# A two-layer SSD / HGRN2 trunk: TensorE's order in the SSD stage written out by hand, diagonal products of two tiles in one run, output projections in halves

## The chip, the cores and the metric

The kernel runs on one core of a Trainium2 chip. The metric is the device time of one execution in microseconds (us), as the median of several runs. Four engines matter here: TensorE (PE in the profile; its weight loads are a row of their own, PEld), VectorE (DVE), ScalarE (ACT) and SyncE (SP), which issues the transfers. Each engine has its own queue of instructions; they wait for each other through semaphores.

## What is computed

The reference is a trunk of two layers over 512 tokens with 1024 features. Layer 0 mixes the tokens with a Mamba-2 SSD mixer, layer 1 with an HGRN2 mixer; each mixer is followed by a layer norm, a squared-ReLU MLP, another layer norm and a gated embedding. The change touches the SSD mixer alone, which is, cut to what matters:

```python
zxbcdt = u @ w_in                                  # z 2048, x 2048, B 512, C 512, dt 32
xbc = silu(causal_depthwise_conv(xbc, conv_w, conv_b))     # x, B and C
dt = softplus(dt + dt_bias); da = dt * -exp(a_log); a_cs = cumsum(da, within a chunk of 128)
decay = segsum_exp(da); xdt = xs * dt
y_diag = einsum(C B^T, decay, xdt)                 # inside a chunk
states = einsum(B, exp(a_cs[last] - a_cs), xdt)    # what a chunk hands on
prev = scan(h * chunk_decay + states)              # over the 4 chunks
y_off = einsum(C, prev, exp(a_cs))                 # what comes from earlier chunks
y = (y_diag + y_off + d_skip * xs) * silu(z)
y = rms_norm(y, over each of 4 groups of 512 features)
return y @ w_out
```

There are 4 groups of 8 heads with 64 features each. B and C belong to a group, everything else to a head.

## The kernel before

**Numbers.** A large product is taken three times (`mm3`, L119 to L121: high by high, high by low, low by high part), each a matmul with 512 columns. Every weight block of 128 x 1024 (a unit) is loaded by SP into `raw`, rounded to its high part by ACT (L113, `whi`) and subtracted to its low part by DVE (L115, `wlo`). Small products (transposes, states, diagonal and carried parts) are single float32 products; each of them is two rows in the profile, except that a transpose is one.

**Tiles of the SSD stage.** The 2048 features are 16 tiles of 128, that is two heads each, and four tiles make a group. For each group there are two projections for B and C (`bc_group`), whose outputs go through the convolution (`conv_silu`, ACT L631, three DVE steps on L634, ACT L635), and `bc_prep`, which transposes B (L660) and forms C B^T masked (TensorE L666, DVE L668, in bank py0). For each tile `xz` makes two projections, x (convolved) and z (Silu, L683). A projection is 8 steps of `mm3`, 24 matmuls. Then `core` does, for one tile:

- the load of its cumulative sums, `csb` (L689), and four transposes of x (L693), which DVE scales to `xw` (L700) and `xdt` (L701);
- the states, three products (L705) into bank pm, and from them the carried states `pv`, a chain of five DVE operations (L712, then L714 and L715 twice), with a chunk decay from ACT (L709);
- the decay matrix `m`: eight DVE steps (L721), an exponential on ACT (L724), a product with C B^T on DVE (L725);
- the diagonal part, eight products (L735) that are 64 output rows wide, into bank py0;
- the carried part, three products (L741) into bank py1;
- y: DVE L748 to L751, then its high part on ACT (L800), its low part on DVE (L801), and the sum of squares (L756, L759).

`rms_group` (L762 to L772) turns a group's sum of squares into the factor `ri`; its products (L767) are 64 x 64. `out_project` multiplies a finished group by its part of the output weights: two halves of 512 output features, four token chunks each, 12 matmuls for each of these eight parts, and DVE adds each part to `acc` (L253).

**What sets the order.** The loop at L783 is written tile by tile: projections of tile j, then `core` of tile j-1, and for some tiles the whole output projection of the group before. That is only the order of priority: on all engines in the SSD stage, TensorE too, a scheduler at compile time decides what goes next, by its own reckoning of when operands are there, and it may put a small product between any two `mm3` matmuls. Two later stages already have TensorE's order written by hand (`manual_schedule`): the value projections and the HGRN2 core.

**Banks and buffers.** PSUM has eight banks here: four take turns for large products (pj), one is for transposes and the group sums (pt), and py0, py1 and pm are single. In the SSD stage x and z tiles have two buffers each, `xdt`, `ecs` and `y` one.

The start (a load of x and of the first four weight blocks, and dt) and everything after the SSD stage is the same in both kernels.

Of the kernel before, what the change touches and what calls it, by code (L numbers as in the profile page):

```python
# [15 lines left out]
P = 128  # L16
# [28 lines left out]
def trunk(ctx: ExitStack, tc, a):  # L45
# [25 lines left out]
    def f32(t):  # L71
        return t.bitcast(F32)

    two = dict(xs=2, sz=2, cv=2, cm=2, cbm=2)
    mlp = dict(r=8, blk=2, sg=2)
    bufs = dict(ssd=dict(two, ss=2), mlp0=mlp, hgrn=dict(two, xs=4, sz=4, cv=4, y=2, pv=2, btok=2, sc=2, scb=2, qd=2), mlp1=mlp)
    phase = []

    def begin(name):
# [539 lines left out]
    def dt_tail():  # L619
# [5 lines left out]
        nc.vector.tensor_copy(t, pt[:, : 3 * P].rearrange("p (i c h) -> p i c h", i=3, c=NCH))  # L625
        return t[:, 0], t[:, 2], t[:, 1]

    def conv_silu(ps, i, out):
# [10 lines left out]
    def projected(i):  # L639

        if i < 4:
            return first[i]
        ps = bank(psj, "pj")
        project(unit(wssd[i - 4]), x_s, ps)
        return ps

    def bc_group(g):
        bcm = []
        for which in range(2):
            ps = projected(10 * g + which)  # L650
            t = tmp(("bm", "cm")[which], [P, T])
            conv_silu(ps, 16 + 4 * which + g, t)
            bcm.append(t)
        return bcm

    def bc_prep(bcm):
# [5 lines left out]
        nc.scalar.copy(btok, pt[:, : 3 * P].rearrange("p (c n) -> p c n", c=3))  # L662
        pc = bank(psy, "py0")
        for c in range(NCH):
            sl = slice(c * P, (c + 1) * P)
            nc.tensor.matmul(pc[:, sl], bm[:, sl], cm[:, sl], start=True, stop=True)  # L666
        cbm = tmp("cbm", [P, T])
        nc.vector.tensor_mul(  # L668
            cbm.rearrange("p (c l) -> p c l", c=NCH), pc.rearrange("p (c l) -> p c l", c=NCH), bc(triu, 1, NCH)
        )  # L670
        return btok, cbm, cm

    toks = []

    def xz(j):
        ps = projected(10 * (j // 4) + 2 + 2 * (j % 4))
        xs = tmp("xs", [P, T])
        conv_silu(ps, j, xs)
        if j == 1:
            toks.extend(dt_tail())  # L680
        ps = projected(10 * (j // 4) + 3 + 2 * (j % 4))
        sz = tmp("sz", [P, T])
        nc.scalar.activation(sz, ps, AF.Silu)  # L683
        return xs, sz

    def core(j, xs, sz, y, toks, btok, cbm, cm, ss=None):
        dt_tok, w_tok, cs_tok = toks
        csb = mk(w4, [P, 2, T], "a")
        nc.sync.dma_start(csb, bass.AP(tensor=csd.tensor, offset=csd.offset + 2 * j * T, ap=[[0, P], [T, 2], [1, T]]))  # L689

        pt = bank(pst, "pt")
        for c in range(NCH):
            nc.tensor.transpose(pt[:, c * P : (c + 1) * P], xs[:, c * P : (c + 1) * P], ident)  # L693
        xdt = tmp("xdt", [P, 8, 64])
        v = pt.rearrange("p (c h q) -> p (c h) q", c=NCH, h=2)
        xdt4 = xdt.rearrange("p (c h) q -> p c h q", c=NCH)
        hs = slice(2 * j, 2 * j + 2)
        ptv = pt.rearrange("p (c h q) -> p c h q", c=NCH, h=2)
        xw = tmp("xw", [P, 3, 2, 64])
        nc.vector.tensor_mul(xw, ptv[:, 0:3], bc(w_tok[:, 0:3, hs], 3, 64))  # L700
        nc.vector.tensor_mul(xdt4, ptv, bc(dt_tok[:, :, hs], 3, 64))  # L701

        pst_ = bank(psm, "pm")
        for c in range(3):
            nc.tensor.matmul(  # L705
                pst_[:, c * P : (c + 1) * P], btok[:, c, :], xw[:, c].rearrange("p h q -> p (h q)"), start=True, stop=True
            )
        cd = mk(sm, [P, 2, NCH], "cd")
        nc.scalar.activation(cd, csb.rearrange("p h (c l) -> p h c l", c=NCH)[:, :, :, P - 1], AF.Exp)  # L709
        pv = tmp("pv", [P, 3, 2, 64])  # L710
        stv = pst_[:, : 3 * P].rearrange("p (c h q) -> p c h q", c=3, h=2)
        nc.vector.tensor_copy(pv[:, 0], stv[:, 0])  # L712
        for c in range(1, 3):
            nc.vector.tensor_mul(pv[:, c], pv[:, c - 1], bc(cd[:, :, c], 2, 64))  # L714
            nc.vector.tensor_add(pv[:, c], stv[:, c], pv[:, c])  # L715

        m = mk(w4, [P, 2, T], "b")
# [9 lines left out]
        ecs = tmp("ecs", [P, 3 * P])  # L727
        for r in range(2):
            rs = slice(64 * r, 64 * r + 64)
            nc.scalar.activation(ecs[rs], csb[rs, r, P:], AF.Exp)  # L730
        yd = bank(psy, "py0")
        for c in range(NCH):
            sl = slice(c * P, (c + 1) * P)
            for r in range(2):
                nc.tensor.matmul(  # L735
                    yd[64 * r : 64 * r + 64, sl], xdt[:, 2 * c + r, :], m[:, r, sl], start=True, stop=True
                )
        ri = None if ss is None else rms_group(ss)
        yo = bank(psy, "py1")
        for c in range(1, NCH):  # L740
            nc.tensor.matmul(  # L741
                yo[:, c * P : (c + 1) * P],
                pv[:, c - 1].rearrange("p h q -> p (h q)"),
                cm[:, c * P : (c + 1) * P],
                start=True,
                stop=True,
            )
        nc.vector.scalar_tensor_tensor(y, xs, dskip[:, j : j + 1], yd, ALU.mult, ALU.add)  # L748
        nc.vector.tensor_mul(ecs, yo[:, P:], ecs)
        nc.vector.tensor_add(y[:, P:], y[:, P:], ecs)  # L750
        nc.vector.tensor_mul(y, y, sz)  # L751
        return ri

    def sq_sum(y, ss):
        sq = tmp("ss" if ss is None else "sq", [P, T])
# [16 lines left out]
        nc.vector.reciprocal(ri, ri)  # L772
        return ri

    def ssd_out(g, s, ri, *after):
        out_project(a["wso"][4 * g : 4 * g + 4], s, False, *after, scale=ri)

    pend = None
    ys = None
    bcm = None  # L780
    prep = None
    outs = []
    for j in range(17):  # L783
        nbcm = bc_group(j // 4) if j % 4 == 0 and j < 16 else None
        cur = xz(j) if j < 16 else None
        if j == 4:
            nc.sync.dma_start(acc, a["x"])
            for c in range(NCH):
                nc.vector.tensor_scalar(acc[:, c, :], acc[:, c, :], ALPHA, None, ALU.mult)
        if pend is not None:  # L790
            i = j - 1
            if i % 4 == 0:
                ys = Split(4)
                ss = None
                prep = bc_prep(bcm)
            y = tmp("y", [P, T])
            due = bool(outs) and (i % 4 == 1 or i == 15) and i != 13
            ri = core(i, *pend, y, toks, *prep, outs[0][2] if due else None)
            w = snw[:, i : i + 1]
            nc.scalar.activation(ys.h(i % 4), y, AF.Copy, scale=w)  # L800
            nc.vector.scalar_tensor_tensor(ys.l(i % 4), y, w, f32(ys.h(i % 4)), ALU.mult, ALU.subtract)  # L801
            ss = sq_sum(y, ss)
            if i % 4 == 3:
                outs.append((i // 4, ys, ss))
            if due:
                ssd_out(*outs.pop(0)[:2], ri)
        if nbcm is not None:
            bcm = nbcm
        pend = cur
# [431 lines left out]
```

## Time and profile before

| | |
|---|---|
| median of 3 runs (lowest, highest) | 1425.94 us (1425.18, 1426.01) |
| the profiled execution's own time | 1424.0 us |
| span in it, from first to last instruction | 1422.2 us |
| granted TensorE clock | 1.000 |
| DVE, ACT busy, share of the span | 74%, 53% |
| DMA read | 174.54 MB, 124 GB/s over the span |

How to read the profile. A row of the timeline has the start, the length, the engine, the line, the operation, the tile written and the tiles read, the sizes, and a count where neighbouring rows of one kind are merged. An idle time before the row stands in brackets with what ended it. Lengths of neighbouring rows overlap, since an engine takes the next instruction while the last is still on its way; what an instruction costs is therefore read from the distance of two starts, not from its length. A busy TensorE is not a TensorE at its peak.

### The profile page before, as it was taken

Reading aid. Unit: us, or ns where it says so; the run is one execution under the profiler, and the core shown is the slowest. Engines: PE = TensorE matmul, PEld = TensorE weight load, DVE = VectorE, ACT = ScalarE, POOL = GpSimd, SP = SyncE. Lnnn points to the kernel's source line nnn. Section 1 sums busy time; section 2 is a strip of 40 time slices with the busy share of each in tenths; the row PEclk is TensorE's granted clock in tenths of the full one; section 3 lists DMA queues with packets and bytes.
Section 4 is the critical chain, followed back from the end, with each engine's and each line's share of the span. In section 5 each row is a group of like instructions: output and inputs, shape, how many; then the busy total and the mean of one; then the engine's idle time right before and its main releaser. Section 6 shows DMA issues by size and latency. Waiting matters only on the chain.

```text
span 1422.2 us, 20042 instructions
## 1 busy us (share of the span) xinstructions
PE 1412.7 (99%) x7869; PEld 1172.5 (82%) x7869; DVE 1055.1 (74%) x1736; ACT 754.2 (53%) x1134; POOL 1.9 (0%) x12
## 2 busy tenths in 40 slices
PE   9999999999999999999999999999999999999998
PEld 7888888888888888888888888877898888888887
DVE  8998687797966767677986576678695867667873
ACT  7776454563265454545545556655555444544641
POOL 0000000000000000000000000000000000000000
PEclk9999999999999999999999999999999999999999
DMA  8432323233333434344621421222163444434231
GB/s 313 138 124 90 120 87 121 102 115 127 145 119 120 161 133 149 133 146 166 214 83 49 133 90 60 75 90 90 46 236 104 148 140 142 149 133 163 89 119 45
DMA packets 49390, 178.00 MB, mean 125 GB/s; under 512 B 5520, under 2 KB 6288, under 8 KB 49168
## 3 DMA queue, kind: packets, MB, share of 16 engines
q1 hardware_dynamic: 49296, 176.73, 36.3%
q8 instruction: 62, 1.02, 0.3%
q14 instruction: 32, 0.26, 0.1%
HBM read 174.54 MB, written 2.16 MB: 124 GB/s over the span
## 4 chain that ended last, share of the span: by engine, by line
PE 94%; DVE 2%; ACT 2%; DMA 1%; issue 0%; ACTq 0%; DVEq 0%
PE pj L119 24%; PE pj L120 24%; PE pj L121 24%; PE py L119 5%; PE py L121 5%; PE py L120 5%; PE py L735 1%; PE pt L233 1%; PE py L741 1%; PE pm L705 1%; DMA raw<-in_wssd 1%; PE py L972 1%; PE pt L693 1%; PE py L1078 1%; DVE wlo L115 0%
## 5 line engine op out<-in xcount | busy, mean ns | idle before, releaser
L113 ACT CAST whi<-raw 128x1024 fp32r<-128x1024 f32 x222 | 232.9, 1051 | 323.5 <-PE pj L120 225.1
L119 PE MATMUL pj<-b,whi 128*128 128x512 f32 (+1 forms) x1006 | 382.3, 381 | 0.7 <-ACT b L237 0.7
L120 PE MATMUL pj<-b,whi 128*128 128x512 f32 (+1 forms) x1006 | 380.3, 378 | 0.0
L121 PE MATMUL pj<-b,wlo 128*128 128x512 f32 (+1 forms) x1006 | 379.3, 377 | 0.0
L115 DVE TENSOR_TENSOR wlo<-raw,whi 128x1024 fp32r<-128x1024 f32 x222 | 270.0, 1221 | 126.4 <-ACT whi L113 124.6
L119 PEld LDWEIGHTS pj<-b,whi 128*128 128x128 f32 x1006 | 188.8, 188 | 34.2 <-ACT b L237 0.9
L121 PEld LDWEIGHTS pj<-b,wlo 128*128 128x128 f32 x1006 | 189.1, 188 | 33.7
L120 PEld LDWEIGHTS pj<-b,whi 128*128 128x128 f32 x1006 | 189.2, 188 | 32.8 <-issue 0.9
L119 PE MATMUL pj<-whi,b 128*128 128x512 f32 x536 | 213.0, 398 | 0.0
L121 PE MATMUL pj<-whi,b 128*128 128x512 f32 x544 | 212.9, 392 | 0.0
L120 PE MATMUL pj<-wlo,b 128*128 128x512 f32 x536 | 210.2, 392 | 0.0
L121 PEld LDWEIGHTS pj<-whi,b 128*128 128x128 f32 x544 | 102.1, 188 | 21.0
L119 PEld LDWEIGHTS pj<-whi,b 128*128 128x128 f32 x536 | 100.7, 188 | 20.7 <-ACT b L1099 0.6
L120 PEld LDWEIGHTS pj<-wlo,b 128*128 128x128 f32 x536 | 100.8, 188 | 19.3
L113 ACT CAST whi<-r 128x1024 fp32r<-128x1024 f32 x72 | 75.8, 1053 | 67.7 <-PE pj L121 38.6
L115 DVE TENSOR_TENSOR wlo<-r,whi 128x1024 fp32r<-128x1024 f32 x72 | 87.7, 1220 | 20.6 <-ACT whi L113 19.9
L121 PE MATMUL py<-whi,b 128*128 128x512 f32 (+1 forms) x250 | 97.0, 388 | 0.0
L120 PE MATMUL py<-wlo,b 128*128 128x512 f32 x224 | 87.1, 389 | 0.0
L119 PE MATMUL py<-whi,b 128*128 128x512 f32 x224 | 87.1, 390 | 0.0
L121 PEld LDWEIGHTS py<-whi,b 128*128 128x128 f32 x250 | 46.9, 188 | 9.7
L634 DVE SCALAR_TENSOR_TENSOR cv<-pj,cst,cv 128x509 f32<-128x509 f32 (+2 forms) x66 | 48.7, 745 | 3.5 <-ACT cv L631 2.8
L119 PEld LDWEIGHTS py<-whi,b 128*128 128x128 f32 x224 | 42.0, 188 | 9.1 <-DVE sg L494 0.3
(292 smaller groups left out, 1850.8 us busy)
## 6 DMA issues: line engine op xcount, KB each, us to landing
raw<-in_w SPq DMA_DIRECT2D x112, 512.0 KB, 3.7
r<-in_w SPq DMA_DIRECT2D x64, 512.0 KB, 4.1
raw<-in_wssd SPq DMA_DIRECT2D x36, 512.0 KB, 3.8
a<-csd SPq DMA_DIRECT2D x16, 512.0 KB, 3.7
raw<-in_wso SPq DMA_DIRECT2D x16, 512.0 KB, 3.6
raw<-in_wg SPq DMA_DIRECT2D x16, 512.0 KB, 3.7
raw<-in_whq SPq DMA_DIRECT2D x16, 512.0 KB, 3.8
raw<-in_whvg SPq DMA_DIRECT2D x14, 512.0 KB, 3.7
```

What stands on the lines that cost most here:

```text
L113: nc.scalar.copy(hi[:, :n], f)
L115: nc.vector.tensor_sub(lo[:, :n], f, f32(hi[:, :n]))
L119: nc.tensor.matmul(out, sh, mh, start=start, stop=False, **kw)
L120: nc.tensor.matmul(out, sh, ml, start=False, stop=False, **kw)
L121: nc.tensor.matmul(out, sl, mh, start=False, stop=stop, **kw)
L233: nc.tensor.transpose(pt[:, j * P : (j + 1) * P], src[:, k * P : (k + 1) * P], ident)
L634: nc.vector.scalar_tensor_tensor(cv[:, d:], ps[:, : T - d], convw[:, i, k : k + 1], cv[:, d:], ALU.mult, ALU.add)
L693: nc.tensor.transpose(pt[:, c * P : (c + 1) * P], xs[:, c * P : (c + 1) * P], ident)
L705: nc.tensor.matmul(pst_[:, c * P : (c + 1) * P], btok[:, c, :], xw[:, c].rearrange("p h q -> p (h q)"), start=True, stop=True)
L735: nc.tensor.matmul(yd[64 * r : 64 * r + 64, sl], xdt[:, 2 * c + r, :], m[:, r, sl], start=True, stop=True)
L741: nc.tensor.matmul(yo[:, c * P : (c + 1) * P], pv[:, c - 1].rearrange("p h q -> p (h q)"), cm[:, c * P : (c + 1) * P], start=True, stop=True,)
L972: nc.tensor.matmul(pcs[r][bs, n * c : n * c + n], kk[r][:, ts], qs, start=True, stop=True)
```

## The change

TensorE's order in the SSD stage is now written out. The stage is cut into nine periods. Each has a list of background work (projections of B and C, of x and z, and halves of output projections, `partial`) which is a sequence of items of three matmuls (one `mm3`): 8 items for a projection, 16 for half an output projection. After a given number of items a small piece is put in. `core` is taken apart into four: `enter` (transposes), `states`, `carried` and `diagonal`. `head(j, n, step)` puts `enter` of tile j after item n, `states` after `n + step`, `carried` after `n + 2 * step`, with 4 as the usual step. `diagonal` is called for two neighbouring tiles at once, the second into bank pm, except for tiles 14 and 15, which have a call each; the factor `ri` of the group before is made in the same place where it is due. The output projections of groups 0 to 2 come as halves in different periods; that of group 3 is as before. x and z tiles get four buffers; `xdt`, `ecs` and `y` get two. The products and their sizes are the same as before; the product with `ecs` now follows the carried part directly.

```diff
-    two = dict(xs=2, sz=2, cv=2, cm=2, cbm=2)
+    two = dict(cv=2, cm=2, cbm=2)
...
+    bufs = dict(ssd=dict(two, xs=4, sz=4, xdt=2, ecs=2, y=2, ss=2), ...
...
-        project(unit(wssd[i - 4]), x_s, ps)
+        hi, lo = unit(wssd[i - 4])
+        for k in range(8):
+            c = slice(k * P, (k + 1) * P)
+            mm3(ps, hi[:, c], lo[:, c], x_s.h(k), x_s.l(k), k == 0, k == 7)
+            if k < 7:
+                yield
         return ps
...
-    def core(j, xs, sz, y, toks, btok, cbm, cm, ss=None):
+    def enter(j):
+        d = tiles[j]
+        d["csb"] = mk(w4, [P, 2, T], "a")
+        nc.sync.dma_start(d["csb"], bass.AP(tensor=csd.tensor, offset=csd.offset + 2 * j * T, ap=[[0, P], [T, 2], [1, T]]))
         pt = bank(pst, "pt")
...
+        nc.vector.tensor_mul(d["xw"], ptv[:, 0:3], bc(w_tok[:, 0:3, hs], 3, 64))
+        nc.vector.tensor_mul(d["xdt"].rearrange("p (c h) q -> p c h q", c=NCH), ptv, bc(dt_tok[:, :, hs], 3, 64))
+    def states(j):
...
+    def carried(j):
...
+        nc.vector.tensor_mul(d["ecs"], yo[:, P:], d["ecs"])
+    def diagonal(js, rms=None):
+        yds = []
+        for n, j in enumerate(js):
+            yd = bank(psm, "pm") if n else bank(psy, "py0")
+            for c in range(NCH):
+                sl = slice(c * P, (c + 1) * P)
+                for r in range(2):
+                    nc.tensor.matmul(
+                        yd[64 * r : 64 * r + 64, sl], tiles[j]["xdt"][:, 2 * c + r, :], tiles[j]["m"][:, r, sl], start=True, stop=True
+                    )
+            yds.append(yd)
+        if rms is not None:
+            groups[rms]["ri"] = rms_group(groups[rms]["ss"])
+        for j, yd in zip(js, yds):
...
+            nc.vector.scalar_tensor_tensor(y, d["xs"], dskip[:, j : j + 1], yd, ALU.mult, ALU.add)
+            nc.vector.tensor_add(y[:, P:], y[:, P:], d["ecs"])
+            nc.vector.tensor_mul(y, y, d["sz"])
...
+    def partial(g, h):
+        units = [unit(a["wso"][4 * g + 2 * h + i]) for i in range(2)]
+        for c in range(NCH):
...
+            for k in range(4):
...
+                if k < 3:
+                    yield
+            d = acc[:, c, h * 512 : (h + 1) * 512]
+            nc.vector.scalar_tensor_tensor(d, ps, groups[g]["ri"][:, c : c + 1], d, ALU.mult, ALU.add)
+            yield
...
+    def period(p, work, at):
+        n = 0
+        for item in work:
+            for _ in item:
+                n += 1
+                for f in at.pop(n, ()):
+                    f()
...
+    def head(j, n, step=4):
+        return {n: [lambda: enter(j)], n + step: [lambda: states(j)], n + 2 * step: [lambda: carried(j)]}
+    both = lambda js, rms=None: [lambda: diagonal(js, rms)]
+    with tc.manual_schedule(engines={mybir.EngineType.PE}):
+        period(0, [bc_group(0), xz(0), xz(1)], {})
+        toks.extend(dt_tail())
+        period(1, [xz(2), xz(3)], {8: [bc_prep], **head(0, 12), **head(1, 22)})
+        period(2, [bc_group(1), xz(4), xz(5)], {1: both((0, 1)), **head(2, 3), **head(3, 14), 26: [bc_prep], 27: both((2, 3)), **head(4, 37)})
+        for p in range(3, 8):
+            i, b = 2 * p - 1, p // 2
+            if p == 7:
+                work = [partial(1, 1), xz(14), xz(15)]
+                at = {**head(i, 1), 18: both((i - 1, i), 2), **head(14, 32, 3), 43: both((14,))}
+            elif p % 2:
+                work = [xz(i + 1), xz(i + 2)]
+                work.insert(1, partial(b - 1, 0))
+                at = {**head(i, 1), 15: both((i - 1, i), b - 1), **head(i + 1, 20)}
+            else:
+                work = [bc_group(b), xz(i + 1), xz(i + 2)]
+                if p == 4:
+                    work.insert(1, partial(0, 1))
+                n = 16 * len(work) - 48
+                at = {**head(i, 1), 14: both((i - 1, i)), 26: [bc_prep], **head(i + 1, 35 + n)}
+            period(p, work, at)
+        period(8, [partial(2, 0), partial(2, 1)], {**head(15, 1), 14: both((15,))})
     h_s, *after = norm(0)
-    g, s, ss = outs.pop(0)
-    ssd_out(g, s, rms_group(ss), *after)
+    out_project(a["wso"][12:16], groups[3]["ys"], False, *after, scale=rms_group(groups[3]["ss"]))
```

More of the change, by code (lines that the diff above doesn't have):

```diff
@@ L72, in f32 @@
         return t.bitcast(F32)
-    two = dict(xs=2, sz=2, cv=2, cm=2, cbm=2)
+    two = dict(cv=2, cm=2, cbm=2)
     mlp = dict(r=8, blk=2, sg=2)
-    bufs = dict(ssd=dict(two, ss=2), mlp0=mlp, hgrn=dict(two, xs=4, sz=4, cv=4, y=2, pv=2, btok=2, sc=2, scb=2, qd=2), mlp1=mlp)
+    bufs = dict(ssd=dict(two, xs=4, sz=4, xdt=2, ecs=2, y=2, ss=2), mlp0=mlp, hgrn=dict(two, xs=4, sz=4, cv=4, y=2, pv=2, btok=2, sc=2, scb=2, qd=2), mlp1=mlp)
     phase = []
@@ L626, in dt_tail @@
         return t[:, 0], t[:, 2], t[:, 1]
+    toks = []
     def conv_silu(ps, i, out):
@@ L643, in projected, with bc_prep @@
         ps = bank(psj, "pj")
-        project(unit(wssd[i - 4]), x_s, ps)
+        hi, lo = unit(wssd[i - 4])
[4 more added lines that the diff above has]
+                yield
         return ps
+    bcm = []
     def bc_group(g):
-        bcm = []
+        new = []
         for which in range(2):
-            ps = projected(10 * g + which)
+            ps = yield from projected(10 * g + which)
             t = tmp(("bm", "cm")[which], [P, T])
             conv_silu(ps, 16 + 4 * which + g, t)
-            bcm.append(t)
-        return bcm
-    def bc_prep(bcm):
+            new.append(t)
+            if g:
+                yield
+        bcm[:] = new
+    prep = []
+    def bc_prep():
         bm, cm = bcm
@@ L670, in bc_prep @@
         )
-        return btok, cbm, cm
-    toks = []
+        prep[:] = btok, cbm, cm
+    tiles = {}
     def xz(j):
[L676 to L684, printed above, removed]
-    def core(j, xs, sz, y, toks, btok, cbm, cm, ss=None):
-        dt_tok, w_tok, cs_tok = toks
-        csb = mk(w4, [P, 2, T], "a")
-        nc.sync.dma_start(csb, bass.AP(tensor=csd.tensor, offset=csd.offset + 2 * j * T, ap=[[0, P], [T, 2], [1, T]]))
+        d = tiles[j] = dict()
+        ps = yield from projected(10 * (j // 4) + 2 + 2 * (j % 4))
+        d["xs"] = tmp("xs", [P, T])
+        conv_silu(ps, j, d["xs"])
+        if j:
+            yield
+        ps = yield from projected(10 * (j // 4) + 3 + 2 * (j % 4))
+        d["sz"] = tmp("sz", [P, T])
+        nc.scalar.activation(d["sz"], ps, AF.Silu)
+        if j:
+            yield
+        if j == 4:
+            nc.sync.dma_start(acc, a["x"])
+            for c in range(NCH):
+                nc.vector.tensor_scalar(acc[:, c, :], acc[:, c, :], ALPHA, None, ALU.mult)
@@ L691, in core @@
+    def enter(j):
+        d = tiles[j]
+        d["csb"] = mk(w4, [P, 2, T], "a")
+        nc.sync.dma_start(d["csb"], bass.AP(tensor=csd.tensor, offset=csd.offset + 2 * j * T, ap=[[0, P], [T, 2], [1, T]]))
         pt = bank(pst, "pt")
         for c in range(NCH):
[L693 to L696, printed above, removed]
+            nc.tensor.transpose(pt[:, c * P : (c + 1) * P], d["xs"][:, c * P : (c + 1) * P], ident)
+        dt_tok, w_tok, _ = toks
+        d["xdt"] = tmp("xdt", [P, 8, 64])
@@ L703, in core @@
+    def states(j):
+        d = tiles[j]
+        csb, cs_tok = d["csb"], toks[2]
+        btok, cbm, cm = prep
         pst_ = bank(psm, "pm")
@@ L705, in core @@
             nc.tensor.matmul(
-                pst_[:, c * P : (c + 1) * P], btok[:, c, :], xw[:, c].rearrange("p h q -> p (h q)"), start=True, stop=True
+                pst_[:, c * P : (c + 1) * P], btok[:, c, :], d["xw"][:, c].rearrange("p h q -> p (h q)"), start=True, stop=True
             )
@@ L715, in core @@
             nc.vector.tensor_add(pv[:, c], stv[:, c], pv[:, c])
[L717 removed]
+        m = d["m"] = mk(w4, [P, 2, T], "b")
         for r in range(2):
@@ L725, in core @@
         nc.vector.tensor_mul(m, m, bc(cbm, 1, 2))
-        ecs = tmp("ecs", [P, 3 * P])
+        d["ecs"] = tmp("ecs", [P, 3 * P])
         for r in range(2):
             rs = slice(64 * r, 64 * r + 64)
[L730 to L738, printed above, removed]
+            nc.scalar.activation(d["ecs"][rs], csb[rs, r, P:], AF.Exp)
+    def carried(j):
+        d = tiles[j]
+        cm = prep[2]
         yo = bank(psy, "py1")
@@ L773, in rms_group @@
         return ri
[L775 to L809, printed above, removed]
@@ new lines, in period @@
+    def period(p, work, at):
[5 more added lines that the diff above has]
+                    f()
+        assert not at, (p, n, at.keys())
+    def head(j, n, step=4):
[23 more added lines that the diff above has]
+        period(8, [partial(2, 0), partial(2, 1)], {**head(15, 1), 14: both((15,))})
```

32 lines of the change are left out of this document (22 added, 10 removed).

## The prediction

> **What bounds the kernel now.** I read the page first, then the busy times by stretch, then the timeline of TensorE around one tile's small products.
>
> ```profile
> span 1422.2 us, 20042 instructions
> ...
> PE 1412.7 (99%) x7869; PEld 1172.5 (82%) x7869; DVE 1055.1 (74%) x1736; ACT 754.2 (53%) x1134; POOL 1.9 (0%) x12
> ```
>
> ```profile
> 18.00:372.00 354.00, 353.78 (x1931) 292.48 (x1932) 291.30 (x548) 205.83 (x272) 0.00 (x0) 1.00 0.37 127
> 45.00:80.00 35.00, 35.00 (x208) 28.67 (x207) 33.20 (x74) 23.15 (x31) 0.00 (x0) 1.00 0.40 133
> 372.00:390.00 18.00, 16.68 (x138) 16.23 (x138) 18.00 (x24) 4.73 (x9) 0.00 (x0) 1.00 0.36 117
> 786.00:1021.00 235.00, 232.37 (x1997) 188.96 (x1996) 158.69 (x434) 133.88 (x302) 1.28 (x4) 1.00 0.26 86
> ```
>
> In the second fence the columns are the stretch, its length, then the busy time of PE, PEld, DVE, ACT and POOL, the granted clock, the DMA share and GB/s. The SSD stage runs from 18 us (the end of the dt products) to about 372 us. TensorE is busy for 353.78 of its 354 us, so the change can't win by filling gaps: 0.22 us of idle time is all there is. DVE is busy for 291.30 us (82%), and for 33.20 of 35 us between 45 and 80 us. So TensorE sets the end of this stage, and DVE is the next limit. A gain has to come from what TensorE's own instructions cost, and that is read from starts:
>
> ```profile
> 94.55 0.39 PE L121 MATMUL pj<-b,wlo 128*128 128x512 f32 x1
> 94.78 0.60 PE L693 MATMUL pt<-cst,xs 128*128 128x128 f32 x4
> 95.13 0.48 PE L119 MATMUL pj<-b,whi 128*128 128x512 f32 x1
> 95.45 0.39 PE L120 MATMUL pj<-b,whi 128*128 128x512 f32 x1
> ...
> 96.14 0.83 PE L705 MATMUL pm<-xw,btok 128*128 128x128 f32 x6
> 96.90 1.09 PE L735 MATMUL py<-b,xdt 128*64 128x128 f32 x16
> 97.93 0.71 PE L741 MATMUL py<-cm,pv 128*128 128x128 f32 x4
> 98.39 0.48 PE L120 MATMUL pj<-b,whi 128*128 128x512 f32 x1
> 98.71 0.39 PE L121 MATMUL pj<-b,wlo 128*128 128x512 f32 x1
> ...
> 100.55 0.38 PE L741 MATMUL py<-cm,pv 128*128 128x128 f32 x2
> 100.69 0.48 PE L120 MATMUL pj<-b,whi 128*128 128x512 f32 x1
> 101.00 0.40 PE L121 MATMUL pj<-b,wlo 128*128 128x512 f32 x1
> ```
>
> A large matmul follows the last one after 0.23 us (94.55 to 94.78). After small products the next large one starts early and is then 0.32 long, so the fair price of a run of small ones is: from its start to the start of the second large matmul behind it, less one 0.23. The four transposes cost 95.45 - 94.78 - 0.23 = 0.44 us, 0.11 each. A single carried product (two rows) costs 101.00 - 100.55 - 0.23 = 0.22, again 0.11 a row. So going from large to small and back costs nothing by itself, and it doesn't matter into how many runs full-width products are cut.
>
> The diagonal run is different. From 96.14 to 98.71 less 0.23 are 2.34 us for 6 + 4 full-width rows (10 x 0.11 = 1.11) and 16 diagonal rows, which leaves 1.23 us for these. They are 64 wide and the two heads of a step fill the two halves of the array; 16 rows in 1.03 us (96.90 to 97.93) are too fast for one after the other. Eight steps at 0.11 are 0.89, so about 0.34 us of each run is a fixed price of going to this shape and back.
>
> **The change part by part.**
>
> *Diagonal parts of two tiles in one run.* Today there are 16 runs, afterwards 9 (seven pairs, tiles 14 and 15 alone). That saves 7 x 0.34 = 2.4 us. If the fixed price were only the visible excess of the step into the run (six L705 rows at 0.11 end at 96.80, the next starts at 96.90, so 0.1), it would be 0.7; if a second tile cost the whole 1.03 that its 16 rows take inside the run, 7 x (1.23 - 1.03) = 1.4. I take 2.4, since it comes from a whole run's starts and agrees best with the 0.11 of all other rows.
>
> *The order of the other pieces.* Transposes, states and carried products are as many as before, and by the 0.11 a row above their number of runs is free in both directions. The output projections are the same 384 matmuls, in halves or whole. The group sums follow the diagonal run as they did. Sum: nothing. One wait goes:
>
> ```profile
> 42.74 0.39 PE L119 MATMUL pj<-b,whi 128*128 128x512 f32 x1
> 43.35 0.66 PE L693 MATMUL pt<-cst,xs 128*128 128x128 f32 x4 [0.22 <-ACT btok L662]
> ```
>
> The first transposes start 0.61 us after the matmul before them where 0.23 is usual; by hand they come four items after `bc_prep`, so that 0.4 us goes. What is late next is the `xw` behind these transposes, for which there are 2.7 us, as below. Together 2.8 us, if nothing new waits.
>
> *What the hand order adds: waits.* A TensorE that takes its instructions in a fixed order stands still when an operand is late, with all matmuls of the projections queued behind it, ready as they are; today the scheduler puts those first. An item is three matmuls, 0.68 us, so `head` gives four items, 2.7 us, from piece to piece. There are three tight places.
>
> (a) `carried` needs the five-step chain on DVE. One tile's chain now, and the start and end of another's:
>
> ```profile
> 97.01 0.29 DVE L712 COPY pv<-pm 128x128 f32<-128x128 f32 x1 [0.44 <-PE pm L705]
> 97.34 0.29 DVE L714 TENSOR_TENSOR pv<-pv,cd 128x128 f32<-128x128 f32 x1
> 97.66 0.29 DVE L715 TENSOR_TENSOR pv<-pm,pv 128x128 f32<-128x128 f32 x1
> 97.87 1.22 DVE L115 TENSOR_TENSOR wlo<-raw,whi 128x1024 fp32r<-128x1024 f32 x1
> ...
> 99.86 0.28 DVE L715 TENSOR_TENSOR pv<-pm,pv 128x128 f32<-128x128 f32 x1
> ```
>
> ```profile
> 71.23 0.83 PE L705 MATMUL pm<-xw,btok 128*128 128x128 f32 x6
> ```
>
> ```profile
> 76.23 0.28 DVE L715 TENSOR_TENSOR pv<-pm,pv 128x128 f32<-128x128 f32 x1
> ```
>
> From the start of the states (96.14) to the end of the chain (100.14) are 4.0 us with one weight split and one step of y in between; in the other tile 71.23 to 76.51, 5.3 us. By hand `carried` starts 0.67 + 2.7 = 3.4 us after the states, and its third product, the only one that needs the last step, 0.45 later: 3.9 us. Undisturbed, the chain is 0.87 to its first step (96.14 to 97.01), four steps of 0.33 and 0.29, so 2.5 us. So it has room for one split (1.2 us) and not for two things. Bounds for 16 tiles: nothing, or 16 x (5.3 - 3.9) = 22 us. I take 0.05 us a tile, 0.8 us, because the step of y and the diagonal run no longer stand at this place.
>
> (b) In period 2 the diagonal run stands one item behind `bc_prep`, and both use bank py0.
>
> ```profile
> 109.08 1.06 PE L666 MATMUL py<-cm,bm 128*128 128x128 f32 x8
> ```
>
> ```profile
> 110.18 0.69 DVE L668 TENSOR_TENSOR cbm<-py,cst 128x512 f32<-128x512 f32 x1 [1.52 <-PE py L666]
> ```
>
> An idle DVE had the bank free at 110.87, 1.8 us after the start of these eight rows, of which the rows themselves take 0.9 and the item 0.68: 0.2 us of wait, and up to 2 with two splits ahead on DVE. I take 0.3.
>
> ```profile
> L801 DVE SCALAR_TENSOR_TENSOR b<-y,cst,b 128x512 fp32r<-128x512 f32 x16 | 12.0, 748 | 5.5 <-ACT b L800 5.5
> L700 DVE TENSOR_TENSOR xw<-pt,toks 128x384 f32<-128x384 f32 x16 | 8.9, 554 | 8.4 <-PE pt L693 8.2
> L750 DVE TENSOR_TENSOR y<-y,ecs 128x384 f32<-128x384 f32 x16 | 8.8, 550 | 0.0
> ```
>
> (c) After a paired diagonal run DVE gets two tiles' y at once, ten operations of 0.55 to 0.75 us by these groups, some 6 us, and `xw` (0.55) of the next tile may stand behind them. In period 2 the transposes come two items later. I take 0.3; the bounds are 0 and 3.
>
> **Sum.** 2.8 saved, 0.8 + 0.3 + 0.3 = 1.4 lost: 1.4 us less. The profiled execution took 1424.0 us, 1.8 around its span, and the median is 1425.94; the difference is put on the median: 1424.5 us. A measurement of this kernel can tell about 0.2% from no change, 2.85 us, so this is within it.
>
> *Other engines.* DVE and ACT do the same operations. The `csb` load goes with `enter` on SP, in the same order among the weight loads; ACT's cover is wide (205.83 of 354 us busy). If the cover on DVE were gone the stage would follow DVE, as it does where the stage ends:
>
> ```profile
> 386.13 0.75 PE L119 MATMUL pj<-b,whi 128*128 128x256 f32 x4 [0.67 <-ACT b L237]
> 387.52 0.66 PE L233 MATMUL pt<-cst,acc 128*128 128x128 f32 x4 [0.65 <-DVE b L238]
> ```
>
> There DVE is busy for 18.00 of 18 us and TensorE idle for 1.3. The change can shift this by its own size, down as well as up; I leave it.
>
> **The rivals.**
>
> *R1, no waits: faster.* The numbers of items leave every operand in time. For it: undisturbed, (a) and (b) fit almost, and DVE has 18% to spare. Against it: the 45 to 80 us stretch, with DVE at 95%. Time: 1425.94 - 2.8 = 1423.1, and 1421.8 if the 1.3 us after the stage went too.
>
> *R2, DVE is late for `carried`: slower.* One mechanism: the chain of (a) is met by more than one foreign operation in most tiles, as in the 5.3 us tile. With the mean of the two tiles above, 4.65, each tile waits 0.75 us: 16 x 0.75 = 12, less 2.8, so 1435; at half of that 1429. It decides from 0.18 us a tile, where the saving is spent. For it: both chains shown are over 3.9 us. Against it: their order is of a DVE whose scheduler knew that TensorE had other things to do.
>
> *R3, the usual waits of an order by hand.* The HGRN2 stage (786 to 1021 us) has such an order and TensorE idle for 2.6 of 235 us. On 354 us that is 4.0: 1425.94 - 2.8 + 4.0 = 1427.1, no change that can be told.
>
> *R4, the clock.* A long wait could cost more than itself. The first matmuls, after the engine had done nothing, are rows of 256 columns at 3.56 / 8 = 0.45 us, twice the 0.22 that 0.11 for 128 columns makes:
>
> ```profile
> 1.45 3.56 PE L153 MATMUL pm<-sq 128*128 128x256 f32 x8 [1.45 <-DVE sq L150]
> ```
>
> One wait after which such a stretch of 3.56 us came again, at half the rate, would lose 1.8 us; four of them, each behind a wait of its own of 0.5, lose 9.2 and give 1425.9 - 2.8 + 9.2 = 1432. [...] The longest idle time quoted here, 0.67 us, left it at 1.00.
>
> **How the numbers follow.** My forecast and R3 are both within 0.2% (1423.1 to 1428.8): 0.27 and 0.15. R1: 0.30. R2: 0.25, R4: 0.03. So faster 0.30, the same 0.42, slower 0.28. The range reaches down to R1's lower end, 1421.8, and up to 1432.5, halfway between R2's two times, which leaves out about 0.15 above. The likeliest case's own range is 1423.1 to 1426.0.
>
> **What would show it.** Right: 9 diagonal runs, the paired ones about 0.9 us longer than a single one; TensorE's idle time in the stage 1 to 2 us, in pieces under 0.5 in front of L741's and L735's successors. R1: idle under 0.5. R2: rows of the carried products with idle times of 0.3 and more, ended by DVE `pv`, in most tiles. Wrong would be: paired runs that cost twice a single one (then nothing is saved), or waits in front of the transposes for x, which I counted as in time, or a changed stretch behind 372 us.

## The result and the profile after

The changed kernel takes 1447.57 us (median of 4 runs, 1446.45 to 1448.71) against 1425.97 for the kernel before (4 runs): a ratio of 1.0153, with a 95% interval of 1.014 to 1.0165. It is 21.6 us slower, 15 us above the upper end of the range. The profiled execution has a span of 1446.8 us, 24.6 more than before.

The page of the changed kernel, and its busy times in the SSD stage (the stage now ends at 396.5 us, where it ended at 372):

```profile
span 1446.8 us, 20044 instructions
...
PE 1421.9 (98%) x7869; PEld 1178.3 (81%) x7869; DVE 1055.4 (73%) x1736; ACT 781.8 (54%) x1155; POOL 1.9 (0%) x12
```

```profile
19.00:396.50 377.50, 362.03 (x1940) 297.71 (x1933) 291.32 (x547) 233.70 (x293) 0.00 (x0) 0.98 0.35 119
```

TensorE does the same 7869 matmuls, DVE the same 1736 instructions in the same time. What is new: TensorE is idle for 15.5 us of the stage (0.2 before), the granted clock is 0.98 (1.00 before), and ACT has 21 instructions more, all of them loads of function tables. Where TensorE waits, from the view of waits (line, tile, for whom; us in total, times, longest):

```profile
PE py L759 <- DVE pv L737: 5.4, 7, 1.7
PE py L679 <- ACT cm L637: 5.1, 2, 2.6
PE pt L712 <- ACT xs L637: 3.9, 3, 3.3
...
PE pm L727 <- DVE xw L718: 0.8, 2, 0.4
...
PE py L778 <- DVE cbm L681: 0.2, 1, 0.2
```

In the new line numbers L759 are the carried products, L679 is C times B, L712 the transposes of x, L727 the states, L778 the diagonal products. All five are small pieces that the hand order put in a fixed place; no large matmul of the stage ever waits for its own operands. One of the seven waits of the carried products, on TensorE and on DVE:

```profile
86.82 0.83 PE L727 MATMUL pm<-xw,btok 128*128 128x128 f32 x6
...
90.26 0.65 PE L759 MATMUL py<-cm,pv 128*128 128x128 f32 x4
92.13 0.49 PE L759 MATMUL py<-cm,pv 128*128 128x128 f32 x2 [1.23 <-DVE pv L737]
```

```profile
88.08 0.28 DVE L736 TENSOR_TENSOR pv<-pv,cd 128x128 f32<-128x128 f32 x1
88.29 1.22 DVE L115 TENSOR_TENSOR wlo<-raw,whi 128x1024 fp32r<-128x1024 f32 x1
89.42 0.74 DVE L636 SCALAR_TENSOR_TENSOR cv<-pj,cst,cv 128x509 f32<-128x509 f32 x1
90.08 0.28 DVE L737 TENSOR_TENSOR pv<-pm,pv 128x128 f32<-128x128 f32 x1
90.28 0.74 DVE L636 SCALAR_TENSOR_TENSOR cv<-pj,cst,cv 128x510 f32<-128x510 f32 x1
90.93 0.28 DVE L736 TENSOR_TENSOR pv<-pv,cd 128x128 f32<-128x128 f32 x1
91.13 0.74 DVE L636 SCALAR_TENSOR_TENSOR cv<-pj,cst,cv 128x511 f32<-128x511 f32 x1
91.79 0.28 DVE L737 TENSOR_TENSOR pv<-pm,pv 128x128 f32<-128x128 f32 x1
```

Between the steps of the chain stand a weight split and all three steps of C's convolution. It ends at 92.07, 5.25 us after the start of the states, where the places allow 3.9. TensorE starts the third product 1.87 us after the first where 0.45 is usual, so the wait costs 1.4 us, of which the bracket counts 1.23: idle time begins only at the modelled end of the matmul before.

Part of the loss is the clock. The busy times of five stretches, the first around the wait just shown:

```profile
92.00:95.40 3.40, 3.27 (x16) 2.73 (x17) 3.40 (x5) 3.09 (x5) 0.00 (x0) 1.00 0.24 94
116.70:120.10 3.40, 3.40 (x10) 2.65 (x9) 1.77 (x3) 3.14 (x4) 0.00 (x0) 0.50 0.62 186
185.00:188.40 3.40, 3.40 (x13) 3.01 (x13) 1.80 (x7) 2.03 (x2) 0.00 (x0) 0.50 0.79 251
280.50:283.90 3.40, 3.40 (x13) 3.01 (x14) 3.10 (x10) 3.36 (x4) 0.00 (x0) 0.51 0.46 160
331.70:335.10 3.40, 3.40 (x11) 2.83 (x11) 2.38 (x3) 2.13 (x2) 0.00 (x0) 0.51 0.54 163
```

After each of the four longest waits (1.71, 2.51, 2.61 and 3.34 us) TensorE ran for 3.4 us at half its clock, 0.50 by these rows. There it is busy all the time, so no idle time tells of it; the starts do:

```profile
115.80 0.49 PE L759 MATMUL py<-cm,pv 128*128 128x128 f32 x2 [1.71 <-DVE pv L737]
...
116.89 0.63 PE L119 MATMUL pj<-b,whi 128*128 128x512 f32 x1
117.32 0.63 PE L120 MATMUL pj<-b,whi 128*128 128x512 f32 x1
```

0.43 us from one large matmul to the next, where 0.23 is usual. The small products are slow there too. By starts, set against the same rows at full clock, the four stretches lose 1.4 to 1.7 us each, 6.4 us in all (C by B and the five large matmuls behind it take 3.75 us here, 184.72 to 188.47, and 2.05 us in the run with C early below, 173.82 to 175.87).

And the saving is there. A paired diagonal run of the changed kernel:

```profile
70.52 0.39 PE L121 MATMUL pj<-b,wlo 128*128 128x512 f32 x1
70.84 1.09 PE L778 MATMUL py<-b,xdt 128*64 128x128 f32 x16
71.77 1.04 PE L778 MATMUL pm<-b,xdt 128*64 128x128 f32 x16
72.74 0.50 PE L119 MATMUL pj<-b,whi 128*128 128x512 f32 x1
73.08 0.40 PE L120 MATMUL pj<-b,whi 128*128 128x512 f32 x1
```

By the prediction's measure it costs 73.08 - 70.84 - 0.23 = 2.01 us, and 0.09 before it (70.52 to 70.84 where 0.23 is usual). There are nine such runs, as foreseen.

### The profile page after: what moved, and what is told of

Its sections match the earlier page's. It is cut to its first block, busy times and chain, and to the rows that moved or that the text cites. A ratio compares the mean times of both kernels' runs of the same rounds, so it can differ in the third digit from the quotient of the medians.

```text
span 1446.8 us, 20044 instructions
## 1 busy us (share of the span) xinstructions
PE 1421.9 (98%) x7869; PEld 1178.3 (81%) x7869; DVE 1055.4 (73%) x1736; ACT 781.8 (54%) x1155; POOL 1.9 (0%) x12
## 4 chain that ended last, share of the span: by engine, by line
PE 88%; DVE 6%; ACT 4%; issue 1%; DMA 1%; SPq 0%; ACTq 0%; DVEq 0%
PE pj L119 22%; PE pj L120 22%; PE pj L121 22%; PE py L119 5%; PE py L121 5%; PE py L120 5%; DVE wlo L115 1%; DVE cv L636 1%; PE py L759 1%; PE py L778 1%; ACT whi L113 1%; PE pm L727 1%; PE pt L233 1%; ACT L637 1%; PE py L1033 1%
```

## The experiments

**The theory** after this profile: the loss is TensorE standing still at places that are earlier than the chains on DVE and ACT behind them, and running at half clock after the longest waits. **Rivals**: the new pieces themselves cost it (two tiles' y at once, buffers, table loads); or DVE and ACT can't deliver at this pace, so that other places would only move the waits.

### The scheduler orders TensorE again

```diff
-    with tc.manual_schedule(engines={mybir.EngineType.PE}):
+    if True:
         period(0, [bc_group(0), xz(0), xz(1)], {})
```

> The changed kernel, with TensorE's order left to the scheduler again in the SSD stage; the pieces, pairs, halves and buffers stay as changed. Theory (the loss is TensorE standing still at places fixed by hand, for the carried states from DVE, the convolved C and x, and half clock behind the longest waits): idle time of TensorE in the stage under 1.5 us, no stretch at half clock, 1422 to 1428 us. Rival (the pieces themselves cost it: two tiles' y at once, more buffers, more table loads on ACT): over 1440 us.

1424.83 us, ratio to the kernel before 0.9993 (0.9984 to 1.0003). TensorE is idle for 0.07 us of the stage and never at half clock (granted clock 1.00). The pieces, pairs, halves and buffers cost nothing that can be seen; ACT has 15 table loads more than in the kernel before, and TensorE waits for none of them. The order alone makes the loss. Six of the seven pairs still stand in one run.

### Later places

```diff
-        period(2, ..., {1: both((0, 1)), **head(2, 3), **head(3, 14), 26: [bc_prep], 27: both((2, 3)), **head(4, 37)})
+        period(2, ..., {2: both((0, 1)), **head(2, 4, 5), **head(3, 16, 5), 29: [bc_prep], 32: both((2, 3)), **head(4, 37, 5)})
...
-                at = {**head(i, 1), 14: both((i - 1, i)), 26: [bc_prep], **head(i + 1, 35 + n)}
+                at = {**head(i, 4, 5), 18: both((i - 1, i)), 31: [bc_prep], **head(i + 1, 36 + n, 5)}
```

> The changed kernel, with the same hand order but later places: states and carried 5 items apart instead of 4, the first transposes of a period after item 4 instead of 1, the B and C preparation after 29 and 31 instead of 26, the transposes of tile 14 after 38 instead of 32, its diagonal part together with tile 15's. Theory (places too early for the chains on DVE and ACT): waits of 22 us in the stage fall under 6, no half clock, 1424 to 1432 us. Rival (DVE and ACT can't deliver at this pace, wherever the places are): waits come back behind the new places, over 1440 us.

The other periods are shifted in the same way, and tiles 14 and 15 now form an eighth pair, here and in all orders with later places. 1431.66 us, ratio 1.0036 (1.0023 to 1.0049): the time is within what the theory gave, but idle time is still 6 us, and there is one stretch at half clock where none was expected (granted clock 0.68 on average from 142.6 to 148.0 us). The waits for C and x are gone, what is left is one kind:

```profile
PE py L759 <- DVE pv L737: 5.3, 5, 1.9
```

### Single diagonal parts in the changed kernel

```diff
-    both = lambda js, rms=None: [lambda: diagonal(js, rms)]
+    both = lambda js, rms=None: [lambda: diagonal(js[:1], None if js[1:] else rms)] + [lambda: diagonal(js[1:], rms)] * len(js[1:])
```

> The changed kernel, with each pair of diagonal parts taken apart again, the second one item (three matmuls) later. Prediction's price of a run (0.34 us for going to this shape and back): seven more runs, 2.4 us more, 1450.0 us, if the waits stay as they are. Rival (no fixed price, the pair saves nothing): 1447.6 us.

1452.1 us, 4.5 more than with pairs, not 2.4. It says little: every part now uses bank py0, the waits moved too (7.7 us for the carried products instead of 5.4), and a price of a fraction of a microsecond can't be read under waits. It was tried again without them, below.

### Priority on DVE and ACT

```diff
         cv = tmp("cv", [P, T])
-        nc.scalar.activation(cv, ps, AF.Identity, ...)
...
+        with tc.high_priority(offset=2 * LEAD):
+            nc.scalar.activation(cv, ps, AF.Identity, ...)
...
         pv = d["pv"] = tmp("pv", [P, 3, 2, 64])
-        nc.vector.tensor_copy(pv[:, 0], stv[:, 0])
...
+        with tc.high_priority(offset=2 * LEAD):
...
+            nc.vector.tensor_copy(pv[:, 0], stv[:, 0])
```

> The changed kernel, TensorE's order untouched; only the convolution's five steps and the chain of the carried states are put ahead of other work on DVE and ACT, by a priority of 200 instructions. If the waits come from the order in which DVE and ACT take their work, they halve at least: under 11 us of wait, 1428 to 1438 us. If DVE and ACT have no time to spare at these places: 1445 us or more.

1438.35 us, ratio 1.0083 (1.0068 to 1.0098), just above the range of the first case. With TensorE's order untouched 9 us are won; idle time falls from 15.5 to 10.3 us, so it does not halve, and of the four stretches at half clock one is left (granted clock 0.999 over the whole execution, 0.995 in the changed kernel):

```profile
PE py L761 <- DVE pv L739: 4.0, 5, 2.2
PE pt L713 <- ACT xs L638: 2.9, 4, 1.5
PE py L680 <- ACT cm L638: 1.7, 2, 1.2
```

So what stands ahead in the queues of DVE and ACT is a good part of it, mostly for C (5.1 to 1.7), little for the carried products.

### Later places and priority

> The later places together with the priority on DVE and ACT. What is left with later places alone is 6.2 us of idle time, nearly all in front of the carried products. If these wait because of the order on DVE, the priority takes half of it or more: 1425 to 1429 us. If the five dependent steps are simply longer than the 5 items given, it stays at 1430 to 1432.

1434.39 us, ratio 1.0057 (1.0043 to 1.0071): worse than later places alone. The carried products now wait 7.1 us in nine places. Neither case was right. Priority for the convolutions and for the chain at once leaves their mutual order as it was; why it came out worse was not followed up.

### Carried products later still

```diff
-    def head(j, n, step=4):
-        return {n: [lambda: enter(j)], n + step: [lambda: states(j)], n + 2 * step: [lambda: carried(j)]}
+    tail = lambda j: [lambda: carried(j)]
+    def head(j, n, first, second):
+        at = {n: [lambda: enter(j)], n + first: [lambda: states(j)]}
+        return at if second is None else {**at, n + first + second: tail(j)}
...
-                at = {**head(i, 4, 5), 18: both((i - 1, i)), 31: [bc_prep], **head(i + 1, 36 + n, 5)}
+                at = {**head(i, 4, 5, 8), 20: both((i - 1, i)), 31: [bc_prep], **(head(8, 50, 5, 8) if p == 4 else head(12, 36, 5, None))}
```

> The later places, with the carried products moved on alone: 8 items after the states instead of 5 (7 to 9, into the next period where it ends before). Theory (each wait is one chain that is longer than its place allows): idle time in the stage under 1.5 us, no half clock, and the saving of the paired diagonal parts shows: 1422.5 to 1425.5 us, against 1426 of the kernel before. Rival (DVE and ACT can't keep the pace): the waits turn up in front of the diagonal parts or the transposes, 1429 us or more.

1423.23 us, ratio 0.9979 (0.997 to 0.9988): faster than both kernels, 2.9 us below the kernel before (1426.16 in the same runs). The rival of capacity is out. Against the first order with later places, the carried products stand 7 to 9 items behind the states instead of 5, the diagonal runs up to 2 items later (few other places move, by at most 2 items), and that is worth 8.4 us: idle time falls from 6.0 to 0.4 us and the stretch at half clock is gone. The stage with almost no idle time left:

```profile
20.00:355.00 335.00, 334.58 (x1854) 278.69 (x1853) 274.22 (x523) 212.55 (x272) 0.00 (x0) 1.00 0.38 126
```

### The same with priority

> The same with the priority for the convolution and the carried states. Theory: no wait is left to take, so within 1 us of the same without priority, 1422 to 1425.5 us. Rival: if it is faster by 2 us or more, places alone didn't settle it; if slower by 2 or more, the priority delays something that was in time.

1424.51 us, ratio 0.9986 (0.9977 to 0.9995), 1.3 us slower than without, where the theory gave 1 us at most and the rival 2 or more. One wait of 1.1 us came in, of the states for `xw`; that the preferred work delays it is likely, but was not followed up. Nothing was left to win.

### Single diagonal parts without waits

> The order with late carried products, with the eight pairs of diagonal parts taken apart (second part one item later). Without waits to hide it this shows the price of a run by itself: 8 x 0.34 = 2.7 us more than with pairs. If a run has no fixed price: the same time within 0.5 us.

1430.01 us, 6.8 more than with pairs. The second part of a pair asked for bank py0 too and waited for the first one's y, 3.2 us in four places, and one transpose behind them waited 0.2 us. So this measured the bank rather than the run:

```profile
PE py L778 <- DVE y L791: 3.2, 4, 1.4
```

With the second part in bank pm, as it is within a pair:

```diff
-            yd = bank(psm, "pm") if n else bank(psy, "py0")
+            yd = bank(psm, "pm") if n or second else bank(psy, "py0")
```

> The pairs taken apart once more in the order with late carried products, this time with the second part in bank pm, as it is within a pair; in the run before it had to wait for bank py0, which the first part still held. If a run has a fixed price of 0.35 us and nothing waits: 8 x 0.35 = 2.8 us more than with pairs, 1426.0 us. If the earlier loss was something else about single parts: 1429 us or more. If a run has no fixed price: 1423.2.

1425.78 us, ratio 0.9999. With pairs the time was 1423.23, 2.55 less, or 2.8 less when each is set against the kernel before in its own runs (1425.9 here, 1426.16 there): 0.32 to 0.35 us for each of the eight pairs. The first of the two parts of one pair (the second, in bank pm from 71.71 on, costs the same):

```profile
69.45 0.40 PE L121 MATMUL pj<-b,wlo 128*128 128x512 f32 x1
69.78 1.09 PE L778 MATMUL py<-b,xdt 128*64 128x128 f32 x16
70.80 0.50 PE L119 MATMUL pj<-b,whi 128*128 128x512 f32 x1
71.14 0.40 PE L120 MATMUL pj<-b,whi 128*128 128x512 f32 x1
```

71.14 - 69.78 - 0.23 = 1.13 and 0.10 in front of it, 1.23; twice that is 2.46 against 2.10 for a pair. So a run's fixed price is 0.36 us by the starts, and 0.32 to 0.35 by the times.

### C early, alone

```diff
-... 20: both((i - 1, i)), 31: [bc_prep], ...
+... 20: both((i - 1, i)), 26: [bc_prep], ...
```

> The order with late carried products, with one thing put back: the preparation of B and C after item 26 instead of 31, in the two periods where the changed kernel waited for the convolved C. Theory (the place is earlier than the convolution's chain): two waits of 2 to 4 us in front of the product of C and B, and half clock behind them, 1428 to 1434 us. Rival (the wait came from the crowd of the other early places): under 1425 us.

1422.9 us, ratio 0.998 (0.997 to 0.9989): no wait at all. My theory was wrong here: the place after item 26, at which the changed kernel lost 5.1 us of idle time, is late enough for C's convolution in this order. On ACT and TensorE (`cv` from the bank, `cm` the convolved C; the first row is the last matmul of C's projection):

```profile
163.62 0.39 PE L121 MATMUL pj<-b,wlo 128*128 128x512 f32 x1
...
164.50 0.76 ACT L633 ACTIVATE cv<-pj,cst 128x512 f32<-128x512 f32 x1
...
171.08 0.63 ACT L637 ACTIVATE cm<-cv 128x512 f32<-128x512 f32 x1
...
173.46 0.70 ACT L795 ACTIVATE b<-y,cst 128x512 fp32r<-128x512 f32 x1
...
173.82 1.06 PE L679 MATMUL py<-cm,bm 128*128 128x128 f32 x8
```

### The transposes of tile 14 early, alone

```diff
-... **head(14, 38, 5, None)
+... **head(14, 32, 5, None)
```

> The order with late carried products, with one thing put back: the transposes of tile 14 after item 32 instead of 38. Theory: one wait of 2 to 4 us for the convolved x of this tile, and half clock behind it, 1426 to 1429.5 us. Rival (it was late because DVE and ACT had fallen behind by then): under 1425 us.

1426.91 us, ratio 1.0006 (0.9996 to 1.0015), 3.7 more. The wait is there, 2.65 us (3.3 in the changed kernel), with no half clock behind it in the profile (granted clock 1.00 from 309 to 313 us, the wait ends at 309.62): with every other piece in its late place, this one is still too early by four items. That it would be so whatever stands ahead is not shown. Here too a diagonal pair, after item 20, precedes, and the y of its two tiles is ahead of x's convolution in ACT's queue (from 300.73; the projection's last matmul starts at 301.14, the convolution at 302.99).

```profile
PE pt L712 <- ACT xs L637: 2.7, 1, 2.7
```

### C early, with its neighbours put back

```diff
-                at = {**head(i, 4, 5, 8), 20: both((i - 1, i)), 26: [bc_prep], ...
+                at = {**head(i, 4, 5, 4), 14: both((i - 1, i)), 26: [bc_prep], ...
```

> As the last run but one (preparation of B and C after item 26, no wait there), with the neighbours put back too in the same two periods: the paired diagonal parts after item 14 instead of 20, just ahead of the end of C's projection at item 16, and the carried products after 13. Theory (the two tiles' y stands ahead of C's convolution on ACT and DVE, and that is why C is late): the two waits of about 2.5 us in front of the product of C and B come back, 1428 to 1433 us. Rival (they came from waits earlier in the stage): no such wait, under 1425 us.

1434.65 us, ratio 1.006 (1.0043 to 1.0077), 1.7 us above the range of the theory. Both waits are back, 2.8 and 2.5 us, the carried products wait 1.1 us in all, and there are two stretches at half clock, of 6.8 and 3.4 us (granted clock 0.996 over the whole execution):

```profile
166.46 0.40 PE L121 MATMUL pj<-b,wlo 128*128 128x512 f32 x1
...
166.98 1.05 ACT L113 CAST whi<-raw 128x1024 fp32r<-128x1024 f32 x1
167.93 0.72 ACT L795 ACTIVATE b<-y,cst 128x512 fp32r<-128x512 f32 x1
...
169.08 0.70 ACT L795 ACTIVATE b<-y,cst 128x512 fp32r<-128x512 f32 x1
169.69 0.76 ACT L633 ACTIVATE cv<-pj,cst 128x512 f32<-128x512 f32 x1
...
173.50 0.49 PE L673 MATMUL pt<-cst,bm 128*128 128x128 f32 x3
...
176.12 0.63 ACT L637 ACTIVATE cm<-cv 128x512 f32<-128x512 f32 x1
...
176.81 2.08 PE L679 MATMUL py<-cm,bm 128*128 128x128 f32 x8 [2.81 <-ACT cm L637]
```

In both orders C's projection ends with item 16, and TensorE reaches the place of `bc_prep` (B's transposes, L673) at the same time, 173.49 and 173.50. But C's convolution begins 5.2 us later with the pair after item 14 (169.69 instead of 164.50), and two things make up this difference.

- 2.8 us come from TensorE itself. The carried products and the diagonal pair stand ahead of the projection's end instead of behind it, so its last matmul starts at 166.46 instead of 163.62. From there to the place are 7.0 us instead of 9.9, for the same number of items.
- 2.4 us stand in ACT's queue. With the pair after item 20 the convolution follows 0.9 us behind this last matmul, and y comes behind it (173.46). With the pair after item 14 it follows after 3.2 us, behind a weight rounding and both tiles' y.

In the order with C early 2.1 us were to spare (`cm` is ready at 171.71, the product starts at 173.82). By this sum neither part alone makes a wait of 2.8 us: the first would leave 0.7 us, the second 0.2. The run with priority, which changes the queues of DVE and ACT alone, fits this: C's two waits there are 1.7 us together, where the changed kernel has 5.1. The changed kernel shows both, too: 7.0 us from the projection's last matmul (174.69) to the place (181.72), with the convolution 2.8 us behind that matmul (177.47). So the number of items at which C's product stands is not the cause of this wait. It is what TensorE no longer has to do between the projection's end and this place, and what stands ahead of the convolution in ACT's queue. The edit moves the carried products and the diagonal pair together; which of the two moves has which share was not tried.

## Why the prediction was wrong

The forecast was 1424.5 us; 1447.57 came. Step by step:

- *What bounds the kernel*: right. TensorE sets the end of the stage, in every run here.
- *The price of a diagonal run, 0.34 us*: right, 0.32 to 0.36. *The rest of TensorE's work costs the same*: right. The sum of 2.8 us saved, "if nothing new waits", is what the order with late carried products shows: 2.9 (1.7 to 4.3 by its interval), of which the eighth pair, not in the forecast, has 0.3.
- *What the hand order adds: waits.* This is the step that failed. I took 1.4 us in all. The stage got some 23 us longer in spite of a saving of 2.8, so waits and what follows them cost about 26.
  - (a) The carried products: I took 0.8 us from bounds of 0 and 22, with the reason that "the step of y and the diagonal run no longer stand at this place". It was true and didn't matter: convolution steps and weight splits took their room. Idle time 5.4 us, and in the order with later places, where they are all that waits, moving these products on, with the pairs behind them, gave 8.4. The two chains that I had quoted, 4.0 and 5.3 us where 3.9 were allowed, both spoke against the value that I chose.
  - (b) Bank py0 behind `bc_prep`: right in size (0.2 us).
  - (c) y of two tiles ahead of other work: I saw the six microseconds on DVE and looked for who waits only at `xw` (0.8 us). The same y stands in ACT's queue ahead of the convolution of C, and the paired run itself stands ahead of the end of C's projection; together they cost 5.1 us of idle time (C early, with its neighbours put back). For the product of C and B the prediction had worked out no chain.
  - Missing: the convolved x of tile 14, 3.3 us. The prediction named "waits in front of the transposes for x, which I counted as in time" as what would make it wrong, and had worked out no chain for them: ACT, three steps on DVE, a table load of 1.28 us and ACT again. It also took ACT's cover as wide from its share, 205.83 of 354 us; a chain doesn't care for the share.
- *R4, the clock*: given 3 chances in 100, which was an estimate, it happened four times: behind waits of 1.7 us (with one of 0.24 us just ahead of it), 2.5, 2.6 and 3.3 us the granted clock was 0.50 for 3.41 us. My sum for R4 (four waits of 0.5, 1.8 us lost after each) was too small in the waits and a little too large after them: a stretch loses 1.4 to 1.7 us.
- *R2* named the right mechanism for one of three chains, and its bound, 1435, was for that one alone. The range ended at 1432.5 (halfway between R2's two times is 1432) because I added no second chain to it, though each of the chains can be late in the same execution.
- *R3*, the idle time of the HGRN2 stage's hand order, 4 us, told nothing of this one: each place has its own slack.

Not settled: why priority made the order with later places worse, and how the 26 us divide exactly: idle time of 15.5 and half clock of 6.4 are 21.9, and of the rest only a part is what idle time doesn't count (1.23 for 1.4 in the wait shown). About 1 us of the two profiles' difference lies ahead of the stage (the first large matmul starts at 8.94 us, 7.73 before); in the profiles of all these kernels it lies between 7.7 and 9.2.

## What to carry to other kernels

An order written by hand on the busiest engine turns every slack that is misjudged into a full stop (15.5 us of idle time in the stage here, 0.2 before), so each fixed place needs its chain worked out in time: from the end of the projection that feeds it, with what TensorE does in between, and with everything that may stand ahead of it in the other engines' queues. The same place, counted in items, was in time in one order and 2.8 us late in another, in which a diagonal pair and its two tiles' y had moved ahead. With the pieces a few items later (1423.23 and 1422.9 us) the 2.9 us are there; with TensorE's order left to the scheduler (1424.83) 1.2, which is not clear of noise. A saving of 0.2% doesn't bear a wait of 3 us.

## What the runs showed of the hardware

The stretches at half clock in the changed kernel last 3.41 us each and begin at 116.7, 185.0, 280.5 and 331.7 us. That is 0.2 to 0.9 us after the ends of the four longest waits of the stage: 1.71, 2.51, 2.61 and 3.34 us, which end at 115.80, 184.72, 280.38 and 331.53 us. The other waits of the stage, up to 1.23 us, have no half clock behind them.

The length of a wait alone doesn't tell whether half clock follows. The 1.9 us wait in the run with later places, with what comes behind it, and the end of the 2.65 us wait of the run with tile 14's transposes early, with what comes behind it:

```profile
142.60:148.00 5.40, 3.52 (x9) 2.88 (x10) 4.01 (x13) 1.27 (x2) 0.00 (x0) 0.68 0.63 190
```

```profile
309.00:313.00 4.00, 3.38 (x17) 2.87 (x18) 3.83 (x12) 3.96 (x6) 0.00 (x0) 1.00 0.39 128
```

In the first the granted clock is 0.68 on average over 5.40 us, in which TensorE is idle for 1.88. Behind the 2.65 us wait, which ends at 309.62, it stays at 1.00, and the large matmuls start 0.23 us apart (310.35 to 310.58). So in these profiles no half clock followed a wait of 2.65 us, and it did follow shorter ones, of 1.71 us (with one of 0.24 us just ahead of it) and 1.9 us. What makes the difference is not shown. Nor is it shown why the ten runs with tile 14's transposes early spread over 5.1 us (1425.1 to 1430.2) and those with C early, without a wait, over 1.65 (1422.29 to 1423.94).
